# Wide products in every pair of the feed-forward part but a layer's first, with two weight sums made in DRAM

## The chip, the cores and the metric

The kernel runs on one core of a Trainium2 chip. The metric is the device time of one execution in microseconds, as the median of several runs of the same program. The core has a matrix engine (TensorE, PE in the profile, PEld for its weight loads), VectorE (DVE), ScalarE (ACT), GpSimd (POOL) and a queue that only issues transfers (SP). Transfers can also be issued by POOL; a transfer that adds to its destination is always issued there in this kernel.

## The reference

Two layers of an encoder over 512 tokens of width 1024, batch 1, in float32. Each layer has three parallel token mixers (differential attention, a convolution module, neighbourhood attention), merged by gates, then a gated feed-forward network and a gated input embedding:

```python
x = x + merged @ w_o[i]
h = rmsnorm(x, norm_ffn[i])
x = x + (jax.nn.silu(h @ w_ffn_gate[i]) * (h @ w_ffn_up[i])) @ w_ffn_down[i]
h = rmsnorm(x, norm_ple[i])
x = x + jax.nn.sigmoid(h @ w_ple_gate[i]) * (p[i] @ w_ple_in[i])
```

The feed-forward width is 2816, which is 22 blocks of 128. The change concerns `h @ w_ffn_gate` and `h @ w_ffn_up`.

## The kernel before, in words

Activations stand transposed, features on the 128 partitions and the 512 tokens in the free dimension. Every float32 operand is split into a high and a low half, and a product is the sum of three: high by high, high by low, low by high. Each weight block is therefore loaded by SP, its high half made by ScalarE (L143) and its low half by VectorE (L157): `split`.

For the feed-forward network, one block of the gate matrix and the block of the up matrix with the same number make a *pair* (`fb`, 0 to 21). Seen as a two by two matrix of halves (a11 and a12 are the halves of the gate block, a21 and a22 those of the up block) that multiplies the two by two matrix of the activations' halves, the pair is computed with seven block products in place of eight, from sums of weights and sums of activations. The weight sums of a pair are s1 = a11 + a21, s2 = a22 + a21, s3 = s1 + a22, s4 = s3 + a12. `seven` (L964) makes one pair:

- SP loads a11 into s1 (L974), a22 into s2 (L975), the gate block into `g` (L976) and a22 into `a22` (L977).
- POOL adds a21 to s1 and to s2 with two accumulating transfers (L979). s1 and s2 lie in one of three tiles (`self.sums[0..2]`, taken in turn), s3 and s4 in a fourth, `self.sums[3]`, that all pairs share.
- VectorE makes s3 and s4 (L995, L999), with hand-made orderings behind other instructions (`behind`).
- ScalarE and VectorE split everything; the halves of s3 and s4 go to one of two tiles, `spare`, by the pair's parity (`pt` for even pairs, `y` for odd ones).
- TensorE makes the products C (a11, later a12), T (s1), A (s3, s2, s4), Q (a22), each over four blocks of 128 rows. Between them ScalarE copies accumulators, C into A and A into Q.

A product has a *wide* form and a *narrow* one, which `product` picks by the accumulator's shape. With a wide accumulator (128 x 2 x 256) four matmuls of 512 columns multiply the high weights by the activations' high and low halves side by side, and four of 256 columns the low weights by the high half; the two halves of the accumulator are added later. With a narrow one (128 x 256) there are twelve matmuls of 256 columns. The argument `twice` says which form a pair has; the product T is narrow in every pair. A wide pair has other evictions after its products: two halves of each accumulator to add instead of one to take.

The pairs run in three parts, `PARTS` (L40): 0 to 7, 8 to 14, 15 to 21; after each part its share of the down projection follows. Before the change a pair is wide if it is odd or if its part isn't the first (L1149). Within a part `sevens_of` interleaves the products of two neighbouring pairs. `early` marks a layer's pair 0.

The order of TensorE's instructions is the program's own (a manual schedule of that engine). The orders of the other engines and queues are made by a planner from priorities, dependencies and its own count of durations; `high_priority` moves a pair's weight work forward. Each engine then runs its instructions in that order. `tick` (L94) is called once in four blocks of products; it advances the attention's units, which are generators. POOL otherwise does little: a power for each norm (L225), such as glu_rc for the norm at the start of a layer, diff_rc for the heads of the differential attention.

Within a layer (`layer`, L434) the order is: gated convolution input, neighbourhood attention (`natten_in`, `natten_v`), differential attention, gates and branches, output projection, feed-forward, embedding.

Of the kernel before, what the change touches and what calls it, by code (L numbers as in the profile page):

```python
# [11 lines left out]
F32 = mybir.dt.float32  # L12
# [3 lines left out]
ALU = mybir.AluOpType  # L16
# [4 lines left out]
P = 128  # L21
# [30 lines left out]
QUARTERS = (2, 4, 6)  # L52
ORDER = (0, 2, 4, 6, 1, 3, 5, 7)
GAP = 144
BACC = dict(dynamic_dma_scratch_size=1024)


# [4 lines left out]
class Net:  # L62
    def __init__(self, nc, tc, a):
        self.nc, self.tc, self.a = nc, tc, a
        self.uid = 0
        self.phase = "pre"
        self.act_set = None
        self.act_now = []
        self.act_prev = []
        self.live = []  # L70
        self.queue = []
        self.free = 0
        self.wait = []
        self.now = 0
        self.chunks = 0
        self.col = self.rb = self.xin = None
# [17 lines left out]
    def tick(self):  # L94

        self.now += 1
        for e in list(self.live):
            while e in self.live and e[0] <= self.now:
                self.step(e)
        if self.queue and max(self.free, self.queue[0][0]) <= self.now:  # L100
            _, gen, ph, gap = self.queue.pop(0)
            self.free = self.now + gap
            old, self.phase = self.phase, ph
            self.run(gen)
            self.phase = old
# [192 lines left out]
    def build(self):  # L298
        nc, tc, a = self.nc, self.tc, self.a
        self.bufs = dict(wr=3, wh=3, wl=3, h=8, qk=2, kh=2, v=4, pt=2, y=5, z=5, x=4, t=7, rp=4,  # L300
                         e=4, a=3, r=2, rb=1, ss=1, sm=8, rc=4, b=2, s=8)
        self.bg, self.w_ahead = BG, 400
        self.pbufs = dict(mm=3, sc=2, tr=2, av=1)
        with tc.tile_pool(name="sb", bufs=1) as self.pool, \
                tc.tile_pool(name="ps", bufs=1, space=PSUM) as self.psum, \
                tc.tile_pool(name="dr", bufs=1, space=DRAM) as dram:
            xs = dram.tile([KD, P, 512], F32, name="xs")
            self.pis = dram.tile([KD, P, 512], F32, name="pis")
            with tc.manual_schedule(engines={mybir.EngineType.PE}):
                h = self.opening()  # L310
                xsrc = a["xT"]
                for i in range(L):
                    h = self.layer(i, h, xsrc, xs)
                    xsrc = xs
# [119 lines left out]
    def layer(self, i, h, xsrc, xs):  # L434
        self.i, self.h = i, h
        zs, cs = [], []
        self.todo = self.taps(zs, cs)
        self.glu(zs)
        if i == 0:
            self.lambdas()  # L440
        yc, ya, yb = [], [], []
        sn, sd = {}, {}
        self.natten_in(0, sn, yc)
        self.drain(self.renorm)
        self.h = self.hs
        self.natten_v(sn)
        last = self.glu_last(zs)
        self.natten_in(1, sn, yc)
        next(last)
        self.natten_in(2, sn, yc)  # L450
        next(last)
        self.natten_in(3, sn, yc)
        acc, gb = [], []
        self.diff_in(0, sd, ya)
        self.diff_v(0, sd)
        self.diff_in(1, sd, ya)
        self.gate_c(acc, 0)
        self.diff_in(2, sd, ya)
        self.diff_v(1, sd)
        self.diff_in(3, sd, ya)  # L460
        for m in range(1, KD):
            self.gate_c(acc, m)
        for m in range(2):
            self.gate_b(gb, m, AF.Copy, None)
        for g in acc + gb:
            self.act(g, g, AF.Sigmoid, table="sigmoid")
        self.branch_c(acc, yc)
        for m in range(2, 4):
            self.gate_b(gb, m, AF.Sigmoid, "sigmoid")
        self.merge_a(ya, acc)  # L470
        conv = self.run(self.conv(cs, yb))
        pairs = self.inputs()
        for m in range(4, KD):
            self.gate_b(gb, m, AF.Sigmoid, "sigmoid")
            for n in ((0, 1), (2,), (3,), ())[m - 4]:
                self.input_block(pairs, n)
        self.drain(conv)
        mg = self.merge_b(yb, acc, gb)
        ws = self.pair_weights(4)
        x, h = self.w_o(mg, xsrc)  # L480
        self.input_pair(ws, pairs, 4)
        h = self.ffn(h, x)
        return self.ple(h, x, xs, self.inputs())
# [45 lines left out]
    def glu_last(self, zs):  # L529

        self.phase = "glu"
        sg = self.sb("t", [P, 512])
        z = self.sb("z", [P, GW + 2 * HALO, GR])
        self.act(sg, self.proj(OFF_GLU + CB + 3 * P), AF.Sigmoid, table="sigmoid")
        yield
        self.phase = "glu"
        self.gated(z, self.proj(OFF_GLU + 3 * P), sg)
        zs.append(z)
        yield

    def taps(self, zs, cs):

# [421 lines left out]
    def seven(self, wg, wu, bs, tags, spare, side, md, first, fb, early, twice):  # L964
# [3 lines left out]
        with self.tc.high_priority(offset=min(self.w_ahead, self.tc.cur_priority - self.p0)):  # L968
            lo, up = slice(0, 512), slice(512, 1024)
            g, a22 = self.sb("wr", [P, 1024]), self.sb("r", [P, 512])  # L970
            sums = self.sums[self.sevens % 3], self.sums[3]
            self.sevens += 1
            s1, s2, s3, s4 = (s[:, q:q + 512] for s in sums for q in (0, 512))
            nc.sync.dma_start(s1, wg[:, lo])  # L974
            nc.sync.dma_start(s2, wu[:, up])  # L975
            nc.sync.dma_start(g, wg)  # L976
            nc.sync.dma_start(a22, wu[:, up])  # L977
            for q in (s1, s2):
                nc.gpsimd.dma_start(q, wu[:, lo], accum_op=ALU.add)  # L979
            ws = {}  # L980

            def halve(hi, lo, src, names):
                i = self.split(hi, lo, src)
                for q, name in enumerate(names):
                    c = slice(q * 512, q * 512 + 512)
                    ws[name] = (hi[:, c], lo[:, c])
                return i

            wide = lambda: (self.sb("wh", [P, 1024], F32R), self.sb("wl", [P, 1024], F32R))
            i = halve(*wide(), g, ("a11", "a12"))  # L990
            if fb == 1:
                self.behind(i, self.held)
            low = halve(self.sb("kh", [P, 512], F32R), self.sb("a", [P, 512], F32R), a22, ("a22",))
            halve(*wide(), sums[0], ("s1", "s2"))
            i = self.tt(s3, s1, a22, ALU.add)  # L995
            self.behind(i, low)
            if first or fb < 3:
                self.behind(i, self.held if fb else self.mark)
            self.tt(s4, s3, g[:, up], ALU.add)  # L999
            i = halve(*spare, sums[1], ("s3", "s4"))  # L1000
            if self.late[fb % 2] is not None:
                self.behind(i, self.late[fb % 2])
                self.late[fb % 2] = None
# [129 lines left out]
    def ffn(self, h, x):  # L1133
# [10 lines left out]
        for part in PARTS:  # L1144
            mids = md8[:len(part)]
            self.sevens_of((self.seven(self.a["w_fg"][i, fb], self.a["w_fu"][i, fb], bs,
                                       (("mm", "mm", "mm"), ("sc", "sc", "av"))[fb % 2],
                                       spare[fb % 2], side[fb % 2], md8[f], part[0] and f < 2,
                                       fb, fb == 0, fb % 2 == 1 or part[0] > 0)  # L1149
                            for f, fb in enumerate(part)), part[0] == 0)  # L1150
            self.flush()
            down = [self.a["w_fd"][i, m][:, part[0] * P:(part[-1] + 1) * P] for m in range(KD)]
            two = [self.ps(("mm", "sc")[part[-1] % 2 == 0]) for _ in range(2)]
            self.pair(two, down[:2], mids, self.cleared)
            for m in range(KD):
                if m < 2:
                    ps = two[m]
                else:
                    ps = self.ps("mm")
                    self.gemm(ps, down[m], mids)  # L1160
                d = self.sb("t", [P, 512])
                self.tt(d, ps, self.rb, ALU.mult)
                self.tt(x[m], x[m], d, ALU.subtract)
                if part is PARTS[-1]:
                    if m in (0, 2):
                        qk = self.parts_of("qk", [2, 512], 2, F32R)
                    hn.append(self.norm_chunk(m, x[m], self.par(i, "ple", m),
                                              qk[m % 2] if m < 4 else "z", st))
# [350 lines left out]
```

## Time and profile before

| | us |
|---|---|
| runs shown | 1759.98, 1759.23, 1758.08 |
| median | 1759.23 |
| the profiled execution | 1758.65 |
| its span, from the first to the last instruction | 1756.9 |

| engine | busy us | share of the span |
|---|---|---|
| TensorE | 1750.2 | 100% |
| TensorE's weight loads | 1507.1 | 86% |
| VectorE | 1405.9 | 80% |
| ScalarE | 954.5 | 54% |
| POOL | 104.0 | 6% |

The layers take about half of the span each. The feed-forward part of the first layer lies at about 490 to 830 us, that of the second at about 1360 to 1700; the attention of the first layer at about 50 to 310 us. Busy shares are means over stages; matmuls overlap one another, so their pace is read from start to start and not from the durations in the rows. In a row of the timeline the first two numbers are the start and the duration in us; "[... <- ...]" at its end is the idle time ahead of it and what ended that. In a row of groups the numbers after the bar are the busy time in us, the mean of one in ns and the idle time ahead. "Landing" is the time from the issue of a transfer to its last byte.

### The profile page before, as it was taken

To read this page: it belongs to the slowest core of one execution; us is meant where nothing else is said; L and a number is where in the kernel's file an instruction comes from. 1 tells how busy PE (TensorE), PEld (TensorE's weight loads), DVE (VectorE), ACT (ScalarE), POOL (GpSimd) and SP (SyncE) were. 2 spreads that over 40 slices of the span, in tenths; PEclk is the share of its full clock that TensorE was granted. 3 is DMA by queue.
4 is the path that set the end of the run, shared out by engine and by line. 5 is a ranking of instruction groups with operands and counts; after the bars stand their busy time and mean duration, and the time that the engine had idled before them with its cause. 6 is when DMAs were issued, how large, how long until landed. Compare 5 with 4: busy or idle time off the path is not lost.

```text
span 1756.9 us, 25630 instructions
## 1 busy us (share of the span) xinstructions
PE 1750.2 (100%) x9282; PEld 1507.1 (86%) x9282; DVE 1405.9 (80%) x2292; ACT 954.5 (54%) x1705; POOL 104.0 (6%) x114
## 2 busy tenths in 40 slices
PE   9999999999999999999999999999999999999998
PEld 7889888888899888888888898888888998888887
DVE  7968887998798687787776688889887875977776
ACT  5566545225576275574545655553366753745654
POOL 0000000000121020100000000000001210101000
PEclk9999999999999999999999999999999999999999
DMA  6575641334767376544446655323256764756332
GB/s 226 162 188 160 162 126 49 108 99 142 233 159 184 119 169 156 144 118 129 154 132 166 192 149 153 111 72 96 95 178 196 183 170 120 180 142 160 94 105 96
DMA packets 114782, 253.85 MB, mean 144 GB/s; under 512 B 16864, under 2 KB 23776, under 8 KB 114656
## 3 DMA queue, kind: packets, MB, share of 16 engines
q1 hardware_dynamic: 101264, 227.83, 42.1%
q0 software_dynamic: 12672, 23.07, 8.1%
q8 instruction: 73, 1.20, 0.3%
q10 hardware_dynamic: 720, 1.31, 0.2%
q14 instruction: 53, 0.43, 0.1%
HBM read 215.46 MB, written 7.34 MB: 127 GB/s over the span
## 4 chain that ended last, share of the span: by engine, by line
PE 99%; DVE 0%; ACT 0%; POOL 0%; issue 0%; POOLq 0%; ACTq 0%; DVEq 0%
PE ffn_sc L1013 6%; PE ffn_mm L1013 4%; PE ffn_mm L180 4%; PE ffn_mm L181 4%; PE ffn_mm L179 4%; PE ffn_sc L1016 3%; PE mergea_mm L181 2%; PE mergea_mm L180 2%; PE mergea_mm L179 2%; PE ffn_mm L1016 2%; PE diff_sc L800 2%; PE diff_mm L180 2%; PE diff_mm L179 2%; PE gatec_mm L180 2%; PE natten_mm L179 2%; PE gatec_mm L179 2%
## 5 line engine op out<-in xcount | busy, mean ns | idle before, releaser
L160 DVE SCALAR_TENSOR_TENSOR conv_z<-glu_z,pre_par,conv_z 128x512 f32<-128x512 f32 x240 | 179.4, 747 | 3.4
L143 ACT ACTIVATE ffn_wh<-ffn_wr 128x1024 fp32r<-128x1024 f32 (+1 forms) x92 | 92.7, 1021 | 103.1 <-PE ffn_mm L180 69.5
L157 DVE TENSOR_TENSOR ffn_wl<-ffn_wr,ffn_wh 128x1024 fp32r<-128x1024 f32 (+1 forms) x92 | 107.1, 1175 | 25.8 <-ACT ffn_wh L143 25.2
L979 POOL DMA_DIRECT2D ffn_qk<-w_fu x88 | 77.9, 984 | 591.4 <-DMA ffn_qk<-w_fu 274.2
L143 ACT ACTIVATE mergea_wh<-mergea_wr 128x1024 fp32r<-128x1024 f32 (+1 forms) x32 | 27.1, 846 | 96.8 <-PE mergea_mm L180 79.5
L157 DVE TENSOR_TENSOR ffn_t<-ffn_mm,wo_rb 128x512 f32<-128x512 f32 (+1 forms) x58 | 36.1, 623 | 51.1 <-PE ffn_mm L181 51.1
L157 DVE TENSOR_TENSOR ffn_wl<-ffn_qk,ffn_wh 128x1024 fp32r<-128x1024 f32 x44 | 53.7, 1221 | 16.6 <-ACT ffn_wh L143 15.9
L143 ACT ACTIVATE ffn_wh<-ffn_qk 128x1024 fp32r<-128x1024 f32 x44 | 46.6, 1058 | 28.2 <-PE ffn_mm L180 16.2
L143 ACT ACTIVATE diff_a<-diff_sc,diff_s 128x512 f32<-128x512 f32 x32 | 22.1, 690 | 72.6 <-DVE diff_s L893 72.6
L179 PE MATMUL ffn_mm<-ffn_v,ffn_wh 128*128 128x512 f32 x132 | 51.4, 389 | 0.0
L180 PE MATMUL ffn_mm<-ffn_v,ffn_wh 128*128 128x512 f32 x132 | 51.4, 389 | 0.0
L181 PE MATMUL ffn_mm<-ffn_v,ffn_wl 128*128 128x512 f32 x132 | 51.3, 389 | 0.0
L179 PE MATMUL ffn_mm<-ffn_y,ffn_wh 128*128 128x512 f32 x132 | 51.3, 389 | 0.0
L180 PE MATMUL ffn_mm<-ffn_y,ffn_wh 128*128 128x512 f32 x132 | 51.3, 389 | 0.0
L181 PE MATMUL ffn_mm<-ffn_y,ffn_wl 128*128 128x512 f32 x132 | 51.3, 389 | 0.0
L143 ACT ACTIVATE natten_wh<-natten_wr 128x1024 fp32r<-128x1024 f32 x24 | 25.4, 1058 | 42.2 <-issue 15.2
L1013 PE MATMUL ffn_sc<-wo_h,ffn_wh 128*128 128x512 f32 x176 | 47.8, 393 | 0.0
L893 DVE TENSOR_REDUCE diff_s<-diff_sc 128x1 f32<-128x512 f32 x64 | 42.1, 681 | 2.2 <-PE diff_sc L800 2.2
L157 DVE TENSOR_TENSOR ffn_t<-ffn_t,ffn_t 128x512 f32<-128x512 f32 x44 | 30.2, 686 | 15.0 <-ACT ffn_t L143 15.0
L225 POOL TENSOR_TENSOR diff_rc<-diff_sm,pre_power 128x4 f32<-128x4 f32 x8 | 8.9, 1116 | 561.1 <-DVE diff_sm L160 502.6
L157 DVE TENSOR_TENSOR ffn_t<-ffn_t,ffn_e 128x256 f32<-128x256 f32 x72 | 39.9, 554 | 2.4 <-ACT ffn_e L143 1.4
L143 ACT ACTIVATE natten_b<-natten_b,natten_s 128x256 f32<-128x256 f32 x64 | 30.4, 500 | 20.3 <-DVE natten_s L719 20.3
(887 smaller groups left out, 6191.4 us busy)
## 6 DMA issues: line engine op xcount, KB each, us to landing
ffn_qk<-w_fu POOLq DMA_DIRECT2D x88, 256.0 KB, 6.5
ffn_wr<-w_fg SPq DMA_DIRECT2D x44, 512.0 KB, 4.6
ffn_wr<-w_fd SPq DMA_DIRECT2D x32, 448.0 KB, 4.0
ffn_r<-w_fu SPq DMA_DIRECT2D x44, 256.0 KB, 2.9
ffn_qk<-w_fg SPq DMA_DIRECT2D x44, 256.0 KB, 3.4
ffn_qk<-w_fu SPq DMA_DIRECT2D x44, 256.0 KB, 3.5
natten_wr<-w_in SPq DMA_DIRECT2D x16, 512.0 KB, 4.2
diff_wr<-w_in SPq DMA_DIRECT2D x16, 512.0 KB, 4.2
```

Source lines behind the costliest of these rows:

```text
L143: i = self.nc.scalar.activation(out, in_, func, **kw)
L157: return self.nc.vector.tensor_tensor(out, a, b, op)
L160: return self.nc.vector.scalar_tensor_tensor(out, a, s, b, op0, op1)
L179: mm(out, wh, ah, start=first, stop=False, **kw)
L180: mm(out, wh, al, start=False, stop=False, **kw)
L181: mm(out, wl, ah, start=False, stop=last, **kw)
L225: nc.gpsimd.tensor_tensor(col, ms, self.power, ALU.pow)
L800: self.nc.tensor.matmul(out, st4[:, u, qs], keys(st), start=first and n == 0, stop=n == 1, **kw)
L893: nc.vector.tensor_reduce(out=m[:, u:u + 1], in_=sc, op=ALU.max, axis=AX.X, negate=True)
L979: nc.gpsimd.dma_start(q, wu[:, lo], accum_op=ALU.add)
L1013: mm(out, wh[:, c], bs[k][b], start=first and k == 0, stop=False, skip_group_check=True)
L1016: mm(out[:, 0], wl[:, c], bs[k][b][:, 0], start=False, stop=k == 3, skip_group_check=True)
```

## The change

Every pair but a layer's first becomes wide. That changes pairs 2, 4 and 6 in each layer. For these three, s3 and s4 are no longer made by VectorE. Three DRAM tiles of 128 x 1024 (`made`) receive them from a generator, `sums_ahead`, that is started after the first projections of the neighbourhood attention and advanced by one transfer at each tick. For each pair it issues on POOL's queue: a copy of a11 into s3, the additions of a21 and of a22, a copy of s3 into s4, and the addition of a12. In the feed-forward part SP then loads both sums at once, 512 KB, into `self.sums[3]`, and the split is as before.

```diff
+MADE = (2, 4, 6)
...
     def tick(self):
         self.now += 1
+        next(self.ahead, None)
...
+            self.made = {f: dram.tile([P, 1024], F32, name=f"made{f}") for f in MADE}
...
         self.natten_in(0, sn, yc)
+        self.ahead = self.sums_ahead()
         self.drain(self.renorm)
...
+    def sums_ahead(self):
+        q, i = self.nc.gpsimd, self.i
+        for fb, o in self.made.items():
+            g, u = self.a["w_fg"][i, fb], self.a["w_fu"][i, fb]
+            s3, s4, lo, up = o[:, :512], o[:, 512:], slice(0, 512), slice(512, 1024)
+            q.dma_start(s3, g[:, lo])
+            yield
+            for w in (u[:, lo], u[:, up]):
+                q.dma_start(s3, w, accum_op=ALU.add)
+                yield
+            q.dma_start(s4, s3)
+            yield
+            q.dma_start(s4, g[:, up], accum_op=ALU.add)
+            yield
...
-            i = self.tt(s3, s1, a22, ALU.add)
-            self.behind(i, low)
-            if first or fb < 3:
-                self.behind(i, self.held if fb else self.mark)
-            self.tt(s4, s3, g[:, up], ALU.add)
+            if fb in MADE:
+                nc.sync.dma_start(sums[1], self.made[fb])
+            else:
+                i = self.tt(s3, s1, a22, ALU.add)
+                self.behind(i, low)
+                if first or fb < 3:
+                    self.behind(i, self.held if fb else self.mark)
+                self.tt(s4, s3, g[:, up], ALU.add)
             i = halve(*spare, sums[1], ("s3", "s4"))
...
-                                       fb, fb == 0, fb % 2 == 1 or part[0] > 0)
+                                       fb, fb == 0, fb > 0)
```

More of the change, by code (lines that the diff above doesn't have):

```diff
@@ L72, in __init__ @@
         self.free = 0
+        self.ahead = iter(())
         self.wait = []
```

## The prediction

> **What bounds the kernel now.** I read the busy totals first, then the chain that ended last, then what TensorE waited for.
>
> ```profile
> span 1756.9 us, 25630 instructions
> PE 1750.2 (100%) x9282; PEld 1507.1 (86%) x9282; DVE 1405.9 (80%) x2292; ACT 954.5 (54%) x1705; POOL 104.0 (6%) x114
> PE 99%; DVE 0%; ACT 0%; POOL 0%; issue 0%; POOLq 0%; ACTq 0%; DVEq 0%
> ...
> PE pre_av L331 <- DVE pre_zeror L404: 1.1, 1, 1.1
> ```
>
> The last line is the whole list of TensorE's waits: one, at the start. From there to the end TensorE has work, the chain of waits runs through it for 99%, and nothing else is ever late. So a change can gain only what it takes out of the matmul stream itself, and it can lose whenever it makes something late. The profiled execution took 1758.65 us with a span of 1756.9, so 1.75 us lie outside; the median of the three runs, 1759.23, is 0.58 above it.
>
> **What a wide pair is worth.** A narrow product is twelve matmuls of 256 columns (L1020 to L1022); a wide one is four of 512 (L1013) and four of 256 (L1016). The columns are the same, 3072. The third product, T, stays narrow in every pair, so six products of a pair change, 24 matmuls. The trace has both kinds, at the same place of the pattern two pairs apart: in the first part, where one of the two pairs is narrow, and in the second part, where both are wide.
>
> ```profile
> 513.28 1.09 PE L1013 MATMUL ffn_sc<-wo_h,ffn_y 128*128 128x512 f32 x4
> ...
> 533.12 1.09 PE L1013 MATMUL ffn_sc<-wo_h,ffn_y 128*128 128x512 f32 x4
> ...
> 626.11 1.09 PE L1013 MATMUL ffn_mm<-wo_h,ffn_pt 128*128 128x512 f32 x4
> ...
> 645.74 1.09 PE L1013 MATMUL ffn_mm<-wo_h,ffn_pt 128*128 128x512 f32 x4
> ```
>
> Narrow and wide together take 533.12 - 513.28 = 19.84 us, two wide ones 645.74 - 626.11 = 19.63. A pair gains 0.21 us by becoming wide. Pairs 2, 4 and 6 change, in two layers: 6 x 0.21 = **1.26 us**, all of it on the path. It is 0.07% of the run; about 0.2% (3.5 us) is what a measurement of this kernel can tell from no change.
>
> That is 8.75 ns for each of the 144 matmuls that go. The Trainium skill (TensorE: Matmul & The Clock Gate, section "Wait — 56ns, not 53.3ns?") gives a fixed cost of about 2.5 ns to a warm matmul, whatever its columns; by that the change would gain 144 x 2.5 ns = 0.36 us and the run would be 1758.9. The trace disagrees, more than threefold, and I go by the trace.
>
> **VectorE and ScalarE in the six pairs.** A wide pair evicts two halves of each accumulator and adds them. ScalarE: two copies of 256 columns become 512, and four of 256 are added. VectorE: two operations of 512 are added (the sum with the broadcast side tile, and the product with the row factors, which replaces two of 256 that then return as additions), and the two sums s3 and s4 go, which come from DRAM now.
>
> ```profile
> L157 DVE TENSOR_TENSOR ffn_qk<-ffn_qk,ffn_r 128x512 f32<-128x512 f32 x6 | 4.1, 683 | 0.0
> L157 DVE TENSOR_TENSOR ffn_qk<-ffn_qk,ffn_wr 128x512 f32<-128x512 f32 x6 | 4.1, 682 | 0.0
> ...
> L157 DVE TENSOR_TENSOR ffn_t<-ffn_t,ffn_e 128x512 f32<-128x512 f32 x3 | 2.1, 688 | 0.1
> L157 DVE TENSOR_TENSOR ffn_t<-ffn_t,wo_rb 128x512 f32<-128x512 f32 x3 | 2.1, 687 | 0.0
> ...
> L143 ACT ACTIVATE ffn_mm<-ffn_mm 128x256 f32<-128x256 f32 x6 | 2.2, 368 | 1.4 <-PE ffn_mm L1022 1.4
> L143 ACT ACTIVATE ffn_sc<-ffn_sc 128x512 f32<-128x512 f32 x3 | 1.7, 582 | 0.0
> ...
> 508.00:528.00 20.00, 20.00 (x148) 18.96 (x147) 19.47 (x30) 14.55 (x26) 3.51 (x4) 1.00 0.69 186
> ...
> 640.00:660.00 20.00, 20.00 (x125) 17.87 (x124) 18.82 (x29) 15.73 (x29) 3.54 (x4) 1.00 0.74 177
> ```
>
> In the stretches the columns are length, then busy PE, weight load, DVE, ACT and POOL, clock, DMA share, GB/s. VectorE: +0.687 + 0.688 - 0.683 - 0.682 = 0.01 us a pair, nothing. ScalarE: 2 x (0.582 - 0.368) + 4 x 0.368 = +1.9 us a pair, which brings 14.55 of 20 us to 16.5 (two pairs, one of them changed). That is above the 15.73 of the second part, where TensorE did not wait, but not at its end. Both cost 0 while TensorE stays busy over them. VectorE with 19.47 of 20 us is the thin place: if the added operations fall ahead of a split that TensorE needs, the price is their 1.37 us, at most once a pair, 8.2 us in all; if the sums that went stood in such a place, nothing is gained, because no wait of TensorE is there to go. I take 0.
>
> **The load of the made sums (SP).** It writes the tile that the pair before used for its own s3 and s4 (`self.sums[3]`, one for all pairs), so it waits for that pair's low split, takes the time of a 512 KB load, and then the two halves are split.
>
> ```profile
> 500.97 1.23 DVE L157 TENSOR_TENSOR ffn_y<-ffn_qk,ffn_y 128x1024 fp32r<-128x1024 f32 x1 [1.12 <-ACT ffn_y L143]
> 513.55 1.22 DVE L157 TENSOR_TENSOR ffn_pt<-ffn_qk,ffn_pt 128x1024 fp32r<-128x1024 f32 x1
> 514.69 0.28 PE L1020 MATMUL ffn_mm<-wo_rp,ffn_pt 128*128 128x256 f32 x1
> ...
> ffn_wr<-w_fg SPq DMA_DIRECT2D x44, 512.0 KB, 4.6
> ...
> 513.00 0.86 POOL L979 DMA_DIRECT2D ffn_qk<-w_fu  x1 [7.36 <-DMA ffn_qk<-w_fu]
> 537.53 1.06 ACT L143 ACTIVATE ffn_wh<-ffn_qk 128x1024 fp32r<-128x1024 f32 x1 [1.00 <-PE ffn_mm L1021]
> ```
>
> For pair 2: tile free at 502.2, landed at 506.8, split by ScalarE and VectorE (1.06 and 1.22) by about 509.1. Before, that split ended at 514.8, when TensorE was at the product that uses it (514.69): the tightest place of the part gets 5.7 us of air. While SP stands at this load for the tile, the next pairs' loads stand behind it, and behind those POOL's additions; such an addition of pair 5 is issued at 513.00 and its sum is split at 537.53, 24 us later. A few us of waiting on SP are covered: 0.
>
> **The fifteen transfers of a layer (POOL).** For each of three pairs, two plain copies and three accumulating ones, each of 256 KB and each depending on the one before, so POOL waits for a landing before it issues the next. No row shows a transfer from DRAM to DRAM; the nearest are the additions of the feed-forward part, and POOL's other work in the neighbourhood.
>
> ```profile
> L979 POOL DMA_DIRECT2D ffn_qk<-w_fu x88: 862/883/1243, 448.3 to 1623.8; - x88
> DMA to landing us min/median/max: 4.0/6.5/10.1
> ...
> 28.99 1.03 POOL L225 TENSOR_TENSOR glu_rc<-glu_sm,pre_power 128x4 f32<-128x4 f32 x1 [27.68 <-DVE glu_sm L221]
> 214.24 1.02 POOL L225 TENSOR_TENSOR diff_rc<-diff_sm,pre_power 128x4 f32<-128x4 f32 x1 [184.21 <-DVE diff_sm L160]
> ...
> 30.59 0.60 PE L229 MATMUL glu_tr<-pre_ident,glu_rc 128*128 128x128 f32 x4
> 50.24 0.39 PE L684 MATMUL natten_mm<-natten_wh,glu_h 128*128 128x512 f32 x1
> ...
> 60.00:170.00 110.00, 110.00 (x621) 96.22 (x620) 83.08 (x179) 71.06 (x162) 0.00 (x0) 1.00 0.64 178
> q0 software_dynamic: 12672, 23.07, 8.1%
> ```
>
> The chain takes 15 x 4.0 = 60 us to 15 x 10.1 = 152 us, 98 by the median. Issued where the code stands (after the first heads' projections, 50.24), it ends between 110 and 202, before POOL's next work at 214.24; what is queued behind it then waits for nothing. The transfer engines spent 8.1% of 1756.9 us on 88 additions, 1.6 us each; 15 more are 24 us, and the share of 0.64 over 110 us becomes 0.86. I take 0 for both, nearest to the median row; the upper end is the first rival.
>
> **Sum.** 1758.65 - 1.26 = 1757.4 in the profiled execution's terms, 1758.0 in the median's. Own range of this case 1756.4 to 1761.
>
> **Rival 1, slower: the planner pulls the chain forward, and a norm waits behind it.** Only TensorE's order is fixed by hand. The others' is planned, and an instruction that nothing holds back is issued as soon as it can be:
>
> ```profile
> L157 DVE TENSOR_TENSOR diff_t<-diff_rp,diff_r x16: 670/683/687, 140.2 to 1097.3; 128x512 f32<-128x512 f32 x16
> ...
> L808 SPq DMA_DIRECT2D diff_r<-rope x4: 328/503/913, 24.7 to 772.7; - x4
> ...
> ffn_qk<-w_fg SPq DMA_DIRECT2D x44, 256.0 KB, 3.4
> ```
>
> The rope tables are first used at 140.2 and loaded at 24.7. The chain's start has no buffer to wait for, and POOL is empty from 1.3 to 28.99. So in the first layer the chain may begin at 1.3 (in the second, as soon as the first layer has loaded its sums, near 510, among POOL's additions, which have the 24 us). POOL is in order: the transfers that the plan puts ahead of glu_rc must be issued first on the chip, and TensorE uses glu_rc 0.6 us after it is made (30.59). If the plan counts 3.4 us a transfer, what plain loads of the same 256 KB take on SP (last row), eight stand ahead of it, and the eighth is issued after seven landings: 1.3 + 7 x 4.0 + 0.9 = 30.2, or with 6.5 us 47.7. TensorE then stands for 1.2 to 18.7 us, 9.6 at 5.2 us: 1759 to 1777, middle 1768. It decides once the chip is some 13% slower than the plan (3.5 of 27.7 us). For it: the rope rows. Against: the plan's own count is not in the trace, and where it is the chip's or longer, glu_rc is not held. Chance 0.30. In the opening the transfers also share the engines with the first loads. The Trainium skill (DMA: Bandwidth & Descriptors, "Issuing engines are not separate DMA queues") says that transfers of all issuers run on the same 16 engines and interleave; no run here shows it for this place. Its fit in "Anatomy of one DMA" (2.0 us + bytes / 436e3, so 2.6 us here) would make the chain 39 us; the rows' least, 4.0, is above it.
>
> **Rival 2, slower: transfers crowd the attention stage.** The 0.86 is a mean; where bursts of head copies meet the chain, a weight load may come late. Half a landing (3 us) in each layer gives 1764. Against: the share stays under 1, and TensorE has no wait there now. Chance 0.05.
>
> **Rival 3, slower: VectorE late in the first part**, half of the 8.2 us above: 1762. Against: the second part bears the same wide pairs with the two sums still on VectorE. Chance 0.05.
>
> **Rival 4: no gain**, if the wide products pay something that the second part doesn't show: 1759.2. Chance 0.10, inside "same".
>
> **Numbers.** Forecast 0.47, with rival 4 0.57 within 0.2%. Slower 0.40: the three slower rivals. Faster by over 0.2% would need 3.5 us where 1.26 are to be had: 0.03. The range goes from the forecast's low end to 1773, past the middle of rival 1, whose upper third stays out, as does its chance of adding to the others: some 0.15.
>
> **What would show it.** Right: TensorE's waits still one line; L1020 to L1022 in the first part only for the first pair and the T products; two pairs of the first part in 19.63 us; POOL's transfers between 50 and 202. Wrong: transfers before 28.99 on POOL, glu_rc later than 29, an idle time of TensorE before L229; s3 of pair 2 later than 514; VectorE at 20 of 20 us.

## The result, and the profile after

The changed kernel takes 1784.84 us (median of five runs: 1784.68, 1784.81, 1784.84, 1789.60, 1790.22) against 1758.47 for the kernel before beside it: a ratio of 1.016 with an interval from 1.0149 to 1.0171, 26.4 us slower. 1758.0 was forecast, 1773 was the upper end of the range. The profiled execution is the one of 1789.60, 30.95 us above the 1758.65 of the profile before; the terms below are terms of that difference. Three of the five runs are some 5 us shorter than the profiled one, and no profile shows which term is smaller in them.

The change of form is there: TensorE has 9138 matmuls instead of 9282, the 144 fewer that were counted, on the page of after:

```profile
PE 1756.2 (98%) x9138; PEld 1504.6 (84%) x9138; DVE 1406.9 (79%) x2292; ACT 962.3 (54%) x1729; POOL 125.9 (7%) x144
```

Its share fell from 100% to 98%, so it waits. The next view is that of TensorE's waits (us in total, times, longest), which held a single line before:

```profile
PE glu_tr L232 <- POOL glu_rc L228: 11.5, 1, 11.5
PE ffn_mm L1037 <- ACT ffn_mm L146: 7.3, 1, 7.3
PE pre_mm L182 <- ACT pre_y L146: 2.1, 1, 2.1
PE ffn_sc L1037 <- ACT ffn_e L146: 1.9, 2, 1.2
PE ffn_sc L1037 <- ACT ffn_av L146: 1.6, 2, 1.1
...
```

Five waits are new: one behind POOL's power glu_rc, one behind ScalarE's copy of an accumulator, three kinds of small ones. (The change moves line numbers: L225 of before is L228, L229 is L232, the wide matmuls are L1037 and L1040, the POOL additions L1000, the chain L552 to L559, SP's load of the made sums L1017.)

Where the time went by stage is read from POOL's powers, which stand at fixed places of the program. Rows by tile, first those of before, then of after; "first to last" are the starts in the two layers:

```profile
L225 POOL TENSOR_TENSOR wo_rc<-wo_sm,pre_power x2: 4007/4008/4008, 496.0 to 1366.0; 128x4 f32<-128x4 f32 x2
L225 POOL TENSOR_TENSOR ffn_rc<-ffn_sm,pre_power x2: 1033/1033/1033, 835.6 to 1705.6; 128x4 f32<-128x4 f32 x2
```

```profile
L228 POOL TENSOR_TENSOR glu_rc<-glu_sm,pre_power x1: 1357/1357/1357, 43.6 to 43.6; 128x4 f32<-128x4 f32 x1
L228 POOL TENSOR_TENSOR wo_rc<-wo_sm,pre_power x2: 4007/4008/4008, 513.1 to 1395.8; 128x4 f32<-128x4 f32 x2
L228 POOL TENSOR_TENSOR ffn_rc<-ffn_sm,pre_power x2: 1032/1032/1032, 865.4 to 1736.6; 128x4 f32<-128x4 f32 x2
```

From the start to wo_rc of the first layer the loss is 513.1 - 496.0 = 17.1 us. The first feed-forward stage (wo_rc to ffn_rc) takes 352.3 where it took 339.6: 12.7 more. The second layer's attention adds nothing (1395.8 - 865.4 = 530.4, as before), its feed-forward stage 1.2 (340.8 against 339.6). 17.1 + 12.7 + 1.2 = 31.0: the whole difference. The forecast had -0.63 for each feed-forward stage and 0 elsewhere.

**The opening, 17.1 us.** POOL's instructions that write `made`, from 0 to 48 us, with the idle time of the engine before them and the landings:

```profile
L555 POOL DMA_DIRECT2D made<-w_fu x6: 808/839/880, 9.1 to 29.5; - x6
L552 POOL DMA_DIRECT2D made<-w_fg x3: 747/862/866, 1.3 to 10.2; - x3
L557 POOL DMA_DIRECT2D made<-made x3: 544/555/567, 24.0 to 37.0; - x3
L559 POOL DMA_DIRECT2D made<-w_fg x3: 820/842/846, 30.5 to 43.0; - x3
...
  DMA made<-w_fu: 19.2, 6
  DMA made<-w_fg: 7.0, 2
  DMA made<-made: 4.6, 2
```

All fifteen transfers of the first layer are issued between 1.3 and 43.0, and only then, at 43.6, POOL makes glu_rc, which it made at 28.99 before. Between them POOL stands for 30.8 us (the idle lines) waiting for transfers of its own chain to land. It is this queue that holds glu_rc, and not its input, which VectorE has ready at 32.56, 11.0 us ahead of glu_rc:

```profile
32.39 0.17 DVE L224 TENSOR_SCALAR glu_sm<-glu_sm 128x4 f32<-128x4 f32 x1
```

TensorE waits 11.5 us for it. The transfers share the engines with the opening's loads as well: the loads of x land in 7.3 to 8.2 us, before in 4.2 to 5.2, and TensorE's last matmul ahead of the stall starts at 33.08 instead of 30.36, 2.7 late. And after the stall TensorE is slow for a while; windows of after, where the column PEclk (the last but two) is the granted clock:

```profile
46.00:50.00 4.00, 4.00 (x11) 3.14 (x11) 3.09 (x5) 1.23 (x2) 0.00 (x0) 0.50 0.15 25
51.00:55.00 4.00, 4.00 (x20) 3.28 (x19) 3.03 (x10) 1.46 (x2) 0.00 (x0) 1.00 0.16 40
```

At a clock of 0.50 eleven matmuls fit into 4 us, at 1.00 twenty. The same place in TensorE's rows, the first of before, the other two of after:

```profile
33.80 0.39 PE L179 MATMUL glu_mm<-glu_v,glu_wh 128*128 128x512 f32 x1
```

```profile
44.98 1.12 PE L232 MATMUL glu_tr<-pre_ident,glu_rc 128*128 128x128 f32 x4 [11.52 <-POOL glu_rc L228]
...
50.88 0.39 PE L182 MATMUL glu_mm<-glu_v,glu_wh 128*128 128x512 f32 x1
```

The matmul that uses glu_rc started at 30.59 before, so it is 14.4 late; the first of glu_mm is 17.1 late, so the slow stretch costs 2.7. The three terms, 2.7 ahead of the stall, 11.7 over it and 2.7 behind it, are the 17.1. The Trainium skill (TensorE: Matmul & The Clock Gate, Part 1) says that the array's clock falls to half after an idle window of some 3.4 us and comes back after about as long a busy one. The fall agrees: the mean granted clock of 0.65 from 34 to 44 us puts it at about 37.0 (an estimate, with 1.00 ahead of it and 0.50 behind), 3.5 us after TensorE's last matmul. The return took 5.7 us of matmuls here, and 2.9 us after the stall of 7.3 us below.

**The first feed-forward stage, 12.7 us.** The chain of the work that ended last, followed back from 600 us, in the stretch that leads up to the stall of 7.3 us (start, us, what; on POOL "issue" is time that the chain puts down to no one):

```profile
519.30 6.49 DMA ffn_qk<-made
...
526.40 0.58 POOL made L552
526.98 3.41 issue
...
530.40 0.82 POOL made L555
531.22 5.57 issue
...
538.43 1.00 POOL ffn_qk L1000
539.43 6.40 issue
...
577.16 5.98 DMA ffn_qk<-w_fu
...
583.23 0.69 DVE ffn_qk L160
...
585.22 0.07 ACT ffn_y L146
...
586.55 0.50 ACT ffn_mm L146
...
587.09 2.08 PE ffn_mm L1037 x4
```

The second layer's chain has nothing to wait for but the tile's last reader, so its first copy goes out at 526.40, as soon as the first layer's pair 2 has loaded its made sums (519.30 + 6.49). From there POOL is a string of waits with the feed-forward part's own additions (L1000) in the same queue. What it waited for is in the view of the instructions that write `made`, from 520 to 610 us:

```profile
  DMA made<-w_fu: 34.6, 6
  DMA made<-made: 11.1, 3
  DMA made<-w_fg: 9.3, 3
```

55 us of standing for its own transfers to land, twelve times; eight of these waits, 40 us, lie ahead of the addition issued at 577.16. Before, that addition (the seventh behind wo_rc) was issued here:

```profile
534.10 1.76 POOL L979 DMA_DIRECT2D ffn_qk<-w_fu  x2 [8.32 <-DMA ffn_qk<-w_fu]
```

With the opening's 17.1 us added that is 551.2, so it is 26.0 us late, more than the 24 us that were taken as cover. It lands at 583.14; VectorE's sum waits for it, ScalarE's split waits for that sum, ScalarE's copy of the accumulator ffn_mm stands behind the split in ScalarE's order, and TensorE waits for the copy. TensorE's waits in this stage come to 10.3 us (7.3, 1.9 behind ffn_e and 1.1 behind ffn_av), and from 587 to 590 the granted clock is 0.50 again; what else the stage lost was not taken apart.

### The profile page after: what moved, and what is told of

Its sections match the earlier page's. It is cut to its first block, busy times and chain, and to the rows that moved or that the text cites. A ratio compares the mean times of both kernels' runs of the same rounds, so it can differ in the third digit from the quotient of the medians.

```text
span 1787.8 us, 25428 instructions
## 1 busy us (share of the span) xinstructions
PE 1756.2 (98%) x9138; PEld 1504.6 (84%) x9138; DVE 1406.9 (79%) x2292; ACT 962.3 (54%) x1729; POOL 125.9 (7%) x144
## 3 DMA queue, kind: packets, MB, share of 16 engines
q8 instruction: 72, 1.18, 0.3%
## 4 chain that ended last, share of the span: by engine, by line
PE 88%; DMA 4%; issue 3%; DVE 3%; ACT 1%; POOL 1%; POOLq 0%; ACTq 0%; DVEq 0%
PE ffn_mm L1037 5%; PE ffn_sc L1037 5%; PE ffn_mm L182 4%; PE ffn_mm L184 4%; PE ffn_mm L183 4%; PE ffn_mm L1040 3%; PE mergea_mm L182 2%; PE mergea_mm L184 2%; PE mergea_mm L183 2%; PE ffn_sc L1040 2%; PE diff_sc L821 2%; DMA made<-w_fu 2%; PE diff_mm L182 2%; PE diff_mm L183 2%; PE gatec_mm L183 2%
## 5 line engine op out<-in xcount | busy, mean ns | idle before, releaser
L1000 POOL DMA_DIRECT2D ffn_qk<-w_fu x88 | 78.7, 988 | 535.4 <-DMA ffn_qk<-w_fu 294.5
L160 DVE TENSOR_TENSOR ffn_t<-ffn_mm,wo_rb 128x512 f32<-128x512 f32 (+1 forms) x46 | 31.1, 677 | 50.6 <-PE ffn_mm L184 50.6
L146 ACT ACTIVATE ffn_wh<-ffn_qk 128x1024 fp32r<-128x1024 f32 x44 | 46.5, 1057 | 24.5 <-PE ffn_mm L183 16.1
L160 DVE TENSOR_TENSOR ffn_t<-ffn_t,ffn_e 128x256 f32<-128x256 f32 x84 | 46.7, 556 | 2.7 <-ACT ffn_e L146 1.4
L228 POOL TENSOR_TENSOR diff_rc<-diff_sm,pre_power 128x4 f32<-128x4 f32 x8 | 8.9, 1116 | 563.3 <-DVE diff_sm L163 504.7
L1037 PE MATMUL ffn_sc<-wo_h,ffn_wh 128*128 128x512 f32 x176 | 47.8, 394 | 0.0
L1037 PE MATMUL ffn_mm<-wo_h,ffn_wh 128*128 128x512 f32 x160 | 43.5, 393 | 0.0
L146 ACT ACTIVATE ffn_y<-ffn_qk 128x1024 fp32r<-128x1024 f32 x22 | 23.3, 1061 | 35.4 <-DVE ffn_qk L160 35.4
```

The costliest lines, as they stand in the source:

```text
L146: i = self.nc.scalar.activation(out, in_, func, **kw)
L160: return self.nc.vector.tensor_tensor(out, a, b, op)
L228: nc.gpsimd.tensor_tensor(col, ms, self.power, ALU.pow)
L1037: mm(out, wh[:, c], bs[k][b], start=first and k == 0, stop=False, skip_group_check=True)
```

## The experiments

Theory A was: both large losses are the order of POOL's queue, into which the planner pulls transfers that nothing holds back. Theory B added that the wide pairs then gain what was forecast; theory C laid the loss on the traffic and the landings, wherever the chain stands. The medians, each beside the kernel before on the same chip (1758.36 to 1758.54), and the lateness of three powers in the profiled execution against the first profile:

| kernel | us, median (lowest to highest) | ratio, interval | wo_rc 1st | ffn_rc 1st | ffn_rc 2nd |
|---|---|---|---|---|---|
| changed | 1784.84 (1784.68 to 1790.22) | 1.016, 1.0149 to 1.0171 | +17.07 | +29.78 | +30.95 |
| sums_alone | 1780.32 (1779.02 to 1784.37) | 1.0129, 1.0115 to 1.0143 | +14.14 | +19.15 | +20.34 |
| pinned_first | 1771.88 (1771.56 to 1772.26) | 1.0077, 1.0062 to 1.0093 | +1.06 | +12.09 | +13.34 |
| pinned | 1761.20 (1758.83 to 1765.81) | 1.0016, 1.0008 to 1.0025 | +0.32 | +1.26 | +2.52 |
| wide_alone | 1757.24 (1756.65 to 1757.60) | 0.9993, 0.9985 to 1.0002 | -0.69 | -1.33 | -1.98 |
| pinned_46 | 1759.30 (1758.37 to 1762.78) | 1.0006, 0.9998 to 1.0015 | +0.29 | -0.35 | -0.97 |
| pinned_late | 1761.20 (1758.64 to 1762.63) | 1.0014, 1.0004 to 1.0023 | +0.37 | +1.18 | +2.12 |
| traffic | 1770.28 (1769.87 to 1771.21) | 1.0067, 1.0054 to 1.0081 | +8.78 | +10.41 | +11.19 |
| serial | 1787.72 (1786.78 to 1790.28) | 1.0168, 1.0154 to 1.0182 | +17.14 | +28.38 | +28.10 |
| quiet_46 | 1758.49 (1757.83 to 1758.76) | 0.9999, 0.9991 to 1.0008 | -0.18 | -0.81 | -1.44 |
| quiet | 1759.54 (1758.11 to 1761.47) | 1.0006, 0.9997 to 1.0015 | -0.07 | -0.23 | +0.85 |
| quiet_own | 1758.58 (1757.81 to 1759.73) | 1.0000, 0.9991 to 1.0008 | -0.33 | -0.69 | -0.86 |

**wide_alone: the wide pairs without the made sums.**

```diff
-MADE = (2, 4, 6)
+MADE = ()
```

> No sums made in DRAM and no chain: VectorE makes s3 and s4 as before, and the first part's even pairs are wide. Theory A (ScalarE, not VectorE, is what the wide pairs press): like the pinned kernel, about 1760.8. Rival (VectorE is the limit, and the made sums are what lets the pairs be wide): slower than the pinned kernel, 1762 or more, with idle time of TensorE behind VectorE's subtractions. Theory B (no engine is pressed): 1757.2.

1757.24 us. TensorE's waits and the powers by tile:

```profile
PE pre_av L335 <- DVE pre_zeror L408: 1.1, 1, 1.1
```

```profile
L228 POOL TENSOR_TENSOR wo_rc<-wo_sm,pre_power x2: 4006/4008/4010, 495.3 to 1364.7; 128x4 f32<-128x4 f32 x2
L228 POOL TENSOR_TENSOR ffn_rc<-ffn_sm,pre_power x2: 1032/1032/1032, 834.3 to 1703.7; 128x4 f32<-128x4 f32 x2
```

Each feed-forward stage is 0.64 us shorter than before (-1.33 + 0.69 and -1.98 + 1.34, the attention of the second layer being the same), where the prediction's working gave 0.63 a layer. Theory B holds and A's extra 1.15 us a layer falls: the wide pairs cost ScalarE and VectorE nothing that TensorE sees, and VectorE can make s3 and s4 beside them. By medians the gain is 1.12 us; its interval doesn't exclude no change, though the highest of wide_alone's eleven runs, 1757.60, is below the lowest of the kernel before beside it, 1757.81. The made sums were not needed for the wide pairs.

**pinned: the chain behind the norm.** Each pair's first copy is ordered behind the layer's norm on POOL (glu_rc in the first layer, ple_rc at 886.8 in the second), and the generator waits until that norm has been issued.

```diff
-            nc.gpsimd.tensor_tensor(col, ms, self.power, ALU.pow)
+            rci = nc.gpsimd.tensor_tensor(col, ms, self.power, ALU.pow)
+            if n == D:
+                self.rci = rci
...
+        if i:
+            self.rci = None
...
+        while self.rci is None:
+            yield
...
-            q.dma_start(s3, g[:, lo])
+            self.behind(q.dma_start(s3, g[:, lo]), self.rci)
```

> The made sums stay, but each pair's first copy is ordered behind the layer's norm on POOL (glu_rc in the first layer, the norm ahead of the second layer in the second), so that the chain runs inside attention, where the code places it. Theory A (the queue's order is the loss, and the wide pairs cost ScalarE time): both large stalls go, and what stays is the 1.15 us a layer that the second layer's feed-forward stage shows: 1758.5 + 2 x 1.15 = 1760.8. Theory B (the queue's order is the whole loss, and the wide pairs then gain as predicted): 1757.2. Theory C (the traffic and the landing of the made sums hurt wherever the chain stands): 1765 or more.

1761.20 us: an order alone gives back 23.6 of 26.4 us. Theory A's number is met, but not for its reason, since wide_alone shows that the wide pairs are free. What is left over wide_alone is 4.0 us, and the runs are 7 us apart. The chain that ended last, from 498 to 512 us of this kernel:

```profile
501.28 1.22 DVE ffn_y L160
...
502.54 6.15 DMA ffn_qk<-made
...
508.71 0.05 ACT ffn_pt L146
508.75 0.92 issue
509.67 0.59 ACT ffn_av L146
...
510.30 1.20 PE ffn_sc L1043 x4
```

Pair 2's load of the made sums is issued when pair 1's split (ffn_y) has freed the one tile, and lands at 508.68. ScalarE's order has the split of those sums (ffn_pt) ahead of the copy of ffn_av, an accumulator of pair 1, and TensorE waits for the copy. In wide_alone that copy started at 505.7:

```profile
L146 ACT ACTIVATE ffn_av<-ffn_sc x1: 582/582/582, 505.7 to 505.7; 128x512 f32<-128x512 f32 x1
```

That was theory D, tried below.

**pinned_first: only the first layer's chain behind the norm** (the ordering above under `if i == 0`).

> Only the first layer's chain is ordered behind the norm; the second layer's is free to run among the first layer's feed-forward pairs. Theory A: the opening gives back its 17.1 us and the feed-forward stage of the first layer keeps its 12.7: 1758.5 + 12.7 + 1.15 = 1772.4. Rival (the chain costs its traffic, not its order, so moving it from the opening into attention only moves the loss): 1780 or more. Rival (the 12.7 us came from the late opening, not from the second chain): 1760 to 1762.

1771.88 us, with theory A's 1772.4 at half a us. The opening is back to +1.06 at wo_rc; the first feed-forward stage still loses 11.0 (12.09 - 1.06), to the same wait:

```profile
PE ffn_mm L1045 <- ACT ffn_mm L146: 7.0, 1, 7.0
```

So the two losses are independent: each chain is paid for where it was pulled to, and the second does not hang on the late opening.

**sums_alone: the free chains, with the first part's even pairs narrow as before.**

```diff
-                                       fb, fb == 0, fb > 0)
+                                       fb, fb == 0, fb % 2 == 1 or part[0] > 0)
```

> The made sums and their free chains as in the changed kernel, but the first part's even pairs keep the narrow products of before. Theory A (chains are the loss, wide pairs cost a little): 1784.8 less up to 2 x 1.15, so 1782.5 to 1784.8, with the POOL stall at glu_tr unchanged at 11.5 us. Theory B (wide pairs gain as predicted): 1784.8 + 1.3 = 1786.1. Rival (the wide products carry most of the loss): under 1770.

1780.32 us, 2.2 below the lowest number expected. Most of the loss is there without a single wide pair added: the made sums carry it. In the profiled execution the first feed-forward stage loses 5.0 instead of 12.7, so the wide pairs may make the same disturbance dearer. That isn't shown: the opening, which the edit doesn't touch, loses 14.1 instead of 17.1 as well, the two profiled executions lie 10.6 us apart and the medians 4.5.

**serial: one chain after the other.** The prediction read the fifteen transfers as one chain, each depending on the one before; in the code only those of one pair do, and the planner had interleaved three chains. Here each pair's first copy is ordered behind the pair before:

```diff
+            c = q.dma_start(s3, g[:, lo])
+            if fb > 2:
+                self.behind(c, e)
...
+            e = q.dma_start(s4, g[:, up], accum_op=ALU.add)
```

> As the changed kernel, but each pair's first copy is ordered behind the last transfer of the pair before, so that POOL has one chain after the other, as the prediction read the code; nothing holds the chain behind the norm. The built order has nine transfers ahead of glu_rc in the first layer instead of fifteen, seven of them waiting for a landing. By the prediction's own formula for its first rival (1.3 + 7 landings of 4.0 to 6.5 + 0.9) glu_rc comes between 30.2 and 47.7. Theory A with the 6.9 us that landings took in the changed kernel's chain: 50, a stall like the 11.5 us or longer. Rival (with no two chains at a time each landing is the 4.0 to 4.8 of an undisturbed one): 30 to 36, a stall of 2 to 6 us, and a total of 1770 to 1776.

1787.72 us; the waits and the power:

```profile
PE glu_tr L232 <- POOL glu_rc L228: 13.7, 1, 13.7
```

```profile
L228 POOL TENSOR_TENSOR glu_rc<-glu_sm,pre_power x1: 1079/1079/1079, 44.2 to 44.2; 128x4 f32<-128x4 f32 x1
```

Nine transfers stand ahead of glu_rc, one more than the prediction's eight, seven of which wait for a landing; glu_rc comes at 44.2, inside the formula's 30.2 to 47.7, but neither at theory A's 50 nor within its rival's 30 to 36, and the total is far from that rival's 1770 to 1776. Fifteen interleaved transfers delayed it as much as nine in a row, because three chains share each wait. For the opening, the misreading of the code changed the count, not the time.

**traffic: the same bytes without the waits.** On top of pinned, POOL issues fifteen plain copies of 256 KB into tensors that nothing reads.

```diff
+        if i == 0:
+            for n in range(15):
+                w = self.a["w_fu" if n % 3 else "w_fg"][i, 2 + n % 6]
+                q.dma_start(self.spill[n], w[:, slice(0, 512)])
```

> As the pinned kernel, and from the opening on POOL issues fifteen plain copies of 256 KB from the weights into fifteen tensors in DRAM that nothing reads: the same bytes out of DRAM from the same queue at the same time as the free chain, but none waits for another. Theory A (POOL's order holds glu_rc, not the traffic): glu_rc no later than 32 and a total of at most 2.5 us above the pinned kernel's 1761.2, the 2.1 us by which the opening loads were late included. Rival (the traffic makes the opening's loss): TensorE late by over 10 us by 60, 1770 or more.

1770.28 us: a miss for theory A, which had at most 1763.7, and on the rival's side. But the mechanism is a third one. Waits and the landings of the opening's loads of x in this kernel:

```profile
POOL glu_rc L228 <- DVE glu_sm L224: 20.0, 1, 20.0
```

```profile
DMA to landing us min/median/max: 5.8/11.5/16.1
```

POOL was idle for 20.0 us ahead of glu_rc, which came at 36.9: its queue held nothing back. The loads of x landed in 5.8 to 16.1 us (in wide_alone 4.1 to 5.1). That made glu_rc 7.9 us late; TensorE stood 4.3 us behind ScalarE's pre_y, which depends on the opening's loads, and its granted clock was 0.87 from 20 to 30 us. Fifteen copies without waits are on their way by 17 us, where the free chain, slowed by its own waits, took until 43 for as many; so this is a denser load than the changed kernel's, in which the opening lost 2.7 us ahead of the stall. Traffic is thus a real cost of transfers pulled into the opening, and the smaller part of it in the changed kernel. How much it would be at the chain's pace without POOL's waits was not tried.

**pinned_46: pair 2 back on VectorE** (`MADE = (4, 6)` in pinned).

> As the pinned kernel, but pair 2 makes its sums on VectorE again; only pairs 4 and 6 load them. Theory D (what is left of the pinned kernel's loss over the kernel with wide pairs alone, 1761.2 - 1757.2, is pair 2's load: it can be issued only when pair 1's split has freed the one tile, lands 6.15 us later, and ScalarE, whose order puts that split ahead of the copy of ffn_av out of PSUM, makes TensorE wait): the waits for ffn_av after 509 and 1380 go, 1757.3 to 1758.3, and the runs lie closer than the pinned kernel's 1758.8 to 1765.8. Rival (each made load costs its share): two thirds of 4.0 stay, 1759.9. Rival (the chain's traffic in attention is what is left): 1760 to 1761.

1759.30 us. TensorE's waits for ffn_av are gone, and the feed-forward stages gain 0.64 and 0.63, all of what the wide pairs are worth: theory D's mechanism is right. The time isn't the 1757.3 to 1758.3 that it gave, though, and the runs are still 4.4 us apart.

**pinned_late: ScalarE's split of the made sums behind the copy.**

```diff
+            def last():
+                i = halve(*spare, sums[1], ("s3", "s4"), self.moved if fb in MADE else None)
...
         self.act(A, C, AF.Copy)
         yield
+        if fb in MADE:
...
+                last()
...
-        self.flush(self.act(Q, A, AF.Copy))
+        self.moved = self.act(Q, A, AF.Copy)
+        self.flush(self.moved)
```

> As the pinned kernel with all three made sums, but ScalarE's split of s3 and s4 of pairs 2, 4 and 6 is ordered behind the copy of the pair before out of PSUM (ffn_av and its like). Theory D: the copy is no longer held, TensorE's wait after 509 and 1380 goes, 1757.3 to 1758.5. Rival (the made sums arrive too late for the products that use them, or hold SP's queue and so the next pairs' loads): 1760 or more, with idle time ahead of the product of s3 or of the next pair's a11.

1761.20 us, no change. The wait only moved: TensorE now stands 0.9 us until 514.89 and 0.9 until 1385.86, behind ScalarE's ffn_e. ScalarE has to wait somewhere for a load that lands late; ordering it later only chooses which copy stands behind.

**quiet_46, quiet, quiet_own: the chain in a quiet stretch.** In pinned and pinned_46 the first layer's chain runs from 29.8 to 57 us; one window of pinned there (the DMA share, 1.03, is the last column but one):

```profile
40.00:50.00 10.00, 10.00 (x45) 8.22 (x45) 9.44 (x19) 4.62 (x7) 2.46 (x4) 1.00 1.03 236
```

The three kernels order the chains behind the layer's fourth diff_rc, at 306.9:

```diff
-            if n == D:
-                self.rci = rci
+            if n == P:
+                self.rcs.append(rci)
...
+            self.behind(q.dma_start(s3, g[:, lo]), self.rcs[3])
```

and quiet_own loads pair 2's made sums into another tile:

```diff
-            sums = self.sums[self.sevens % 3], self.sums[3]
+            sums = self.sums[self.sevens % 3], self.own if fb == 2 else self.sums[3]
...
+        self.own = md8[6].rearrange("p a b -> p (a b)").bitcast(F32)
```

> Pairs 4 and 6 alone load made sums, as in the kernel pinned_46, but each chain is ordered behind the layer's fourth diff_rc on POOL (306.9 before), ahead of the quietest stretch of the DMA engines, instead of behind the first norm (28.99), after which the first layer's chain and attention's loads together keep them busy at 1.02 to 1.03 of one. Theory E (what pinned_46 lost against wide pairs alone, 1759.3 against 1757.2 with runs 4.4 us apart, is the chain's traffic among attention's loads): 1757.2 to 1757.6, the runs within 1.5 us. Rival (the loads of pairs 4 and 6 cost it, in runs that the one profile does not show): 1759 again, as widely spread.

> All three pairs load made sums, and the chains stand behind the fourth diff_rc. Theories D and E: only pair 2's load is left, which moved ffn_rc of the two layers by 1.58 and 1.90 us against wide pairs alone: 1757.2 + 3.5 = 1760.7. Rival (pair 2's load is late because the chain's transfers go on beside it, or because of attention's crowding): 1757.3 to 1758.5.

> As the kernel quiet, but pair 2's made sums are loaded into a tile of their own (that of pair 6's result, free until then), so that the load need not wait until pair 1's split has freed the one tile for s3 and s4. Theory D (the tile makes the load late, and the late load holds ScalarE's queue): 1757.2 to 1757.8. Rival (a made sum costs pair 2 something wherever it is loaded: SP's queue, ScalarE's order): 1759 or more.

quiet_46: 1758.49, the runs 0.9 us apart instead of 4.4: with pairs 4 and 6 alone the spread went with the chain's place beside attention's loads, as theory E has it, and moving the chain is worth 0.8 us. But 1.25 over wide_alone stay, where 0 to 0.4 was expected. The feed-forward stages gain 0.63 and 0.63 as they should. Between the profiled executions, 1.58 us apart, 0.5 lies in the opening by the powers, and 1.04 come after the last ffn_rc (the span ends 0.40 before that of the first profile, where ffn_rc was 1.44 ahead). Part of that is seen on SP: the last two transfers of the output are issued 0.76 us apart, from 1751.81, where wide_alone has 0.43, from 1751.00. pinned_46 loses the same behind its last ffn_rc (0.97 ahead there, 0.1 behind at the end) and has the same 0.76; the kernels that load made sums for pair 2 as well, and those that load none, have 0.42 or 0.43. Why stays open, as do the tenths of the opening, which differ between kernels whose openings are the same.

quiet: 1759.54, between theory D's 1760.7 and its rival's, the runs 3.4 us apart. By medians pair 2's load costs 1.0 us over quiet_46. But quiet doesn't have quiet_46's 1.04 at the end: by the powers its two feed-forward stages are 2.2 us longer together than those of wide_alone or quiet_46, and those of pinned 3.5. So the late load costs between 2 and 3.5 us there, by when it lands, and the medians hide about 1 us of it.

quiet_own: 1758.58, 1.0 below quiet, but not the 1757.2 to 1757.8 of theory D. The load was issued at 499.8 instead of 502.2 (quiet), and still ScalarE waited for it:

```profile
L1022 SPq DMA_DIRECT2D ffn_y<-made x1: 327/327/327, 499.8 to 499.8; - x1
...
  ACT ffn_pt L146: 1.8, 1
```

By the powers its feed-forward stages are 0.75 us longer than those of wide_alone, where quiet's are 2.2: the shared tile is most of the load's cost. For the rest there is the landing of 5.8 us; whether an earlier load would take it away was not tried.

None of the kernels with made sums beats the one that has none. wide_alone is the fastest of all, 1757.24 against 1758.36 for the kernel before, and its interval still allows for no change.

## Why the prediction was wrong, step by step

- **What a wide pair is worth: right.** 1.26 us was forecast for six pairs; the feed-forward stages of wide_alone, and those of pinned_46 and quiet_46, are shorter by 0.63 to 0.64 each, 1.27 to 1.28 in all.
- **VectorE and ScalarE in the six pairs, priced at 0: right.** wide_alone has no wait of TensorE behind either, though VectorE still made both sums. Rival 3 did not come.
- **The fifteen transfers of a layer, priced at 0: the step that failed.** It took the transfers at the place where the code issues them, after 50 us. The planner issued the first at 1.3. The rope tables, loaded 115 us ahead of their use, had been quoted as the sign of that, and against it stood only that the plan's own count isn't in a trace; yet it got 0.30. pinned proves the step: an order on the first copies gives back 23.6 us.
- **Rival 1 named the mechanism and was too short in its sum.** It had a stall of 1.2 to 18.7 us, 9.6 in the middle; the stall was 11.5. It left out what the stall brings (2.7 us of half clock after it) and named the traffic of the opening without a price (2.7); with both the opening lost 17.1. Its margin of 3.5 us is smaller by its own terms: 27.7 - 0.9 - 7 x 3.4 = 3.0. Its eight transfers ahead of glu_rc were nine in a row in serial, fifteen interleaved in the changed kernel.
- **The second layer's chain, taken as covered by 24 us: failed by 13.3 us** (12.7 lost where 0.63 was to be gained). It was foreseen to start near 510 and started at 526.40, the same place with the opening's 17.1 us added. The 24 us were one addition's distance from its use, in a queue that otherwise held additions only. The chain does not delay one addition by one landing: every landing it waits for delays all later ones, and at 577.16 the addition was 26.0 us late.
- **The load of the made sums, priced at 0 with 5.7 us of air: failed.** In the first layer of pinned the landing was 6.15 us, not 4.6. Worse, the air was measured up to the product that uses the sums, while the instruction that waits, ScalarE's split, had a copy behind it that TensorE needed at 509 and not at 514.7. The changed kernel's second layer, which loses 1.2 as pinned's does, has a wait of the same kind, 0.5 us. In the profiled feed-forward stages it costs 2.2 us (quiet) to 3.5 (pinned) for the two layers; the medians show 1.0 (quiet against quiet_46) and 1.9 (pinned against pinned_46), because the kernels with pairs 4 and 6 alone lose 1.0 at the end. So the small gain would have been lost even with the chain in its place.
- **Rival 2, transfers that crowd the attention: small.** 0.8 us between pinned_46 and quiet_46, and most of the spread of pinned_46's runs; that it is the crowding, and not another effect of the chain's place, is argued. quiet, with pair 2's load, still spreads by 3.4 us.

## What to carry to other kernels

A transfer into a DRAM tensor that nothing has used yet has no buffer that holds it back, so a planner may issue it as early as the program allows, and on a queue that runs in order every wait for one of its landings is a wait for all that stands behind: where the code is written says nothing, an explicit order behind an instruction of the same queue does. For any work that is made to wait, look past its own consumer to the instructions that the plan has put behind it on the same engine; their deadlines are the ones that count. And try the half of a change that needs no new resource alone first: here it was the whole gain.

## What the runs showed of the hardware that was not expected

- TensorE at half clock after a wait: 0.50 from 46 to 50 us after the stall of 11.5 us, shown above. That wait cost 2.7 us more than its own length.

- The landings of the transfers that wrote and read `made` in the changed kernel, from the list of DMA issues (KB each, median us to landing): longer than the 3.0 to 3.5 of the feed-forward part's plain loads of 256 KB there, and, for the load on SP, than the 4.6 and 5.2 of weight blocks of the same 512 KB. In quiet_46, with two chains in a quieter stretch, those that write `made` landed in 5.3 and 5.0 us in the medians of the two layers; how much is crowding and how much the kind of transfer stays open.

```profile
made<-w_fu POOLq DMA_DIRECT2D x12, 256.0 KB, 6.9
...
ffn_qk<-made SPq DMA_DIRECT2D x6, 512.0 KB, 6.9
```
